# The second layer's heads in groups of two pairs instead of pair by pair

## The chip, the cores and the metric

The kernel runs on one core of a Trainium2 chip. The metric is the device time of one execution in microseconds. Before the change three runs gave 348.47, 349.83 and 350.31; their median is 349.83 us.

## The reference, cut to what matters

Two layers work on 256 tokens of width 1024, all in 32-bit floats. The first layer (a state-space half and a gated linear attention half) is the same before and after. The second layer is this, with 16 heads of width 64; with 256 tokens there is a single block of keys, so what is left of the block-sparse attention is ordinary causal attention:

```python
def moba_layer(x, norm_w, w_in, w_out):
    h = rms_norm(x, norm_w)
    u = h @ w_in                              # 1024 x 4096
    q, k, v, z = split_cols(u, (1024,) * 4)   # 16 heads of 64 each
    s = (q * 64 ** -0.5) @ k.T                # by head, 256 x 256
    p = softmax(where(key <= query, s, -inf))
    o = (p @ v) * silu(z)                     # silu(z) is the gate
    return x + o @ w_out                      # then a last rms_norm
```

## The kernel before, in words

A product of two 32-bit matrices is made of three fast ones: each operand is split into a high part in a reduced 32-bit format (`h_...`, `...hi`) and a low rest (`l_...`, `...lo`), and `mm3` (line 161) queues high x high, high x low and low x high into the same sum. A weight piece of 128 x 1024 numbers comes by one DMA, is split by ScalarE (high part, line 78) and VectorE (rest, line 79), and is then used once. There are four buffers for raw pieces and seven for split ones; pieces are fetched in the order of a list, `pieces`.

Eight pairs of heads are worked on in turn (`for pr in range(8)`). A pair has three projection blocks of 24 matmuls each, written to tiles called `pp`: q, k, and the gate z. After q and k, a generator `co_attn` is started for the pair. It runs beside the projections: `yield 2600` means that its next step is queued when TensorE has been given another 2600 ns of work by the program's own count (`spend`, `due`). The order on TensorE's queue is thus fixed when the program is built. The steps of `co_attn` are:

- scores, tiles `as`: one head of the pair uses the upper 64 rows of the 128 x 128 array and the other the lower 64 rows, so the two run side by side. The first 128 queries are multiplied in full precision, the others by three fast products.
- on VectorE the masked row minimum (line 710), on ScalarE the exponential (line 712), on VectorE the reciprocal of the sum and the rescaling (lines 714 and 716);
- transposes of the probabilities, tiles `ptp`: six full-array matmuls against a unit matrix, copied to `pT` by ScalarE (line 724);
- products with the values, tile `ao`: each head uses 64 columns of the array. VectorE multiplies with the gate (`og`, line 735), ScalarE and VectorE split the result into `oghi` and `oglo` (lines 736 and 737), which are row block `pr` of the last projection's input.

The last projection (tiles `pf`) adds up eight such row blocks. For three of its four tiles the first seven blocks (`lead`) are queued before the generators are drained, the eighth afterwards. In PSUM, `pp` and `pf` share four banks, and the mixers' tiles `as`, `ptp` and `ao` four others.

The lines that do the two steps in question are

```python
for j, r in enumerate(rows):                                   # rows: 0-63, 64-127
    mm(sps[j][:, 0:P], qt[0][r, 0:P], kt[0][r, 0:P])           # scores, full precision
for i, (a_, b_) in enumerate(((1, 1), (1, 2), (2, 1))):
    for j, r in enumerate(rows):
        mm(sps[j][:, P:3 * P], qt[a_][r, :], kt[b_][r, :], i == 0, i == 2)
...
for j, r in enumerate(rows):
    mm(ops[r, 0:T], va[:, 0, hc[j]], pTs[j][:, 0:T], True, False)
```

A full-precision matmul has two records in the trace, a fast one has one.

Of the kernel before, what the change touches and what calls it, by code (L numbers as in the profile page):

```python
# [35 lines left out]
# columns of the packed constants  # L36
# [4 lines left out]
# columns of the packed matrices of shape  # L41
# [5 lines left out]
def trunk(ctx, tc, xT_d, x_d, cst_d, mat_d, gw2_d, fn_d, wa_d, wb_d, wc_d, wv_d, wp_d, wf_d, out_d):  # L47
# [21 lines left out]
    # ------------------------------------------------------------------ weights  # L69
# [50 lines left out]
    for j in range(24):  # L120
        plan(("p", j), wp_d[j], KB, P)
# [49 lines left out]
    # keep the tensor engine's clock up until the first operands arrive  # L171
    warm = cpool.tile([P, T], F32R, name="warm")
# [5 lines left out]
    # ------------------------------------------------------------------ inputs  # L178
# [3 lines left out]
    gw2 = cpool.tile([16, 512], F32, name="gw2")  # L182
# [68 lines left out]
    # ------------------------------------------------------------------ even in-projection  # L251
# [65 lines left out]
    def co_first(ps):  # L317
# [12 lines left out]
        # softplus of the step sizes, by the series of artanh  # L330
# [31 lines left out]
        # gate logits -> cumulated log decay (times 16)  # L362
# [18 lines left out]
    # convolution and silu  # L381
# [74 lines left out]
    # gated linear attention  # L456
# [126 lines left out]
    # ------------------------------------------------------------------ gate of the state-space half  # L583
# [37 lines left out]
    # ------------------------------------------------------------------ even out-projection  # L621
# [13 lines left out]
    def gemm_tt(name, hi8, lo8, tag):  # L635
        """Token-major product, one token tile after the other: yields each when it is done."""
# [46 lines left out]
    # ------------------------------------------------------------------ second layer  # L683
# [12 lines left out]
    def co_attn(pr, qt, kt, ops):  # L696
        yield DL["at0"]
        sps = [pm(f"as{pr}_{j}") for j in range(2)]
        for j, r in enumerate(rows):
            mm(sps[j][:, 0:P], qt[0][r, 0:P], kt[0][r, 0:P])  # L700
        for i, (a_, b_) in enumerate(((1, 1), (1, 2), (2, 1))):
            for j, r in enumerate(rows):
                mm(sps[j][:, P:3 * P], qt[a_][r, :], kt[b_][r, :], i == 0, i == 2)
        pts = [tmp.tile([P, 3 * P], F32, name=f"pt{pr}_{j}", tag="t1d") for j in range(2)]
        for j in range(2):
            pt = pts[j]
            nm = sm.tile([P, 2], F32, name=f"nm{pr}_{j}", tag="nm")
            sme = sm.tile([P, 2], F32, name=f"sme{pr}_{j}", tag="sme")
            for tt, cs in halves:
                V.tensor_tensor_reduce(out=pt[:, cs], in0=sps[j][:, cs], in1=mask[:, cs], scale=rq[:, tt:tt + 1],  # L710
                                       scalar=3e38, op0=ALU.add, op1=ALU.min, accum_out=nm[:, tt:tt + 1])
                S.activation(pt[:, cs], pt[:, cs], AF.Exp, scale=-1.0, bias=nm[:, tt:tt + 1],
                             accum_out=sme[:, tt:tt + 1])
            V.reciprocal(sme, sme)
            for tt, cs in halves:
                V.tensor_scalar(pt[:, cs], pt[:, cs], sme[:, tt:tt + 1], None, op0=ALU.mult)
        yield DL["at2"]
        pTs = []
        for j in range(2):
            tp = pm(f"ptp{pr}_{j}")  # L720
            for i in range(3):
                tr(tp[:, i * P:i * P + P], pts[j][:, i * P:i * P + P])
            pT = tmp.tile([P, 3 * P], F32, name=f"pT{pr}_{j}", tag="t3")
            S.activation(pT, tp[:, 0:3 * P], AF.Copy)
            pTs.append(pT)
        yield DL["at3"]
        hc = [slice(64 * (2 * pr + j), 64 * (2 * pr + j) + 64) for j in range(2)]
        for j, r in enumerate(rows):
            mm(ops[r, 0:T], va[:, 0, hc[j]], pTs[j][:, 0:T], True, False)
        for j, r in enumerate(rows):  # L730
            mm(ops[r, P:T], va[:, 1, hc[j]], pTs[j][:, T:3 * P], False, True)
        while ("z", pr) not in env:
            yield 300
        og = tmp.tile([P, T], F32, name=f"og{pr}", tag="t1f")
        V.tensor_tensor(og, ops[:, 0:T], env[("z", pr)], op=ALU.mult)
        S.activation(oghi[:, pr, :], og, AF.Copy)
        V.tensor_sub(oglo[:, pr, :], og, oghi[:, pr, :].bitcast(F32))

    for pr in range(8):
        qk = []  # L740
        for i in range(2):
            ps = gemm_fm(("p", 3 * pr + i), h1hi, h1lo, f"pp{pr}_{i}")
            t_ = tmp.tile([P, T], F32, name=f"qk{pr}_{i}", tag=("t1a", "t1c")[i])
            n_ = (P, T)[i]
            hi = big.tile([P, n_], F32R, name=f"qkh{pr}_{i}", tag=(("cbT0", "cbT1"), ("qs", "ks"))[i][pr % 2])
            lo = big.tile([P, n_], F32R, name=f"qkl{pr}_{i}", tag=(("s3", "s4"), ("bc", "gs"))[i][pr % 2])
            if i == 0:
                S.activation(t_[:, 0:P], ps[:, 0:P], AF.Copy)
                S.activation(hi, ps[:, P:T], AF.Copy)
                V.tensor_sub(lo, ps[:, P:T], hi.bitcast(F32))  # L750
            else:
                V.tensor_tensor(t_, ps, rb1, op=ALU.mult)
                S.activation(hi, t_, AF.Copy)
                V.tensor_sub(lo, t_, hi.bitcast(F32))
            qk.append((t_, hi, lo))
        ops = pm(f"ao{pr}")
        spawn(co_attn(pr, *qk, ops))
# [134 lines left out]
```

## Time and profile before

| what | value |
|---|---|
| median of three runs | 349.83 us |
| span of the profiled execution | 347.5 us |
| TensorE busy (matmuls) | 335.5 us, 97% of the span |
| VectorE busy | 263.5 us, 76% |
| ScalarE busy | 217.5 us, 63% |
| HBM read | 54.63 MB, 160 GB/s over the span |
| share of the chain that ended last on TensorE | 85% |
| of it projections of the second layer (`pp`) | 21% |

The span runs from the first to the last instruction of the profiled execution; the profile has no time for that execution beyond its span. A matmul's record begins when its operands are being fetched and lasts longer than its place in the queue, so records of neighbours overlap, and what a matmul costs is read from the distance between starts. PE is TensorE, DVE VectorE, ACT ScalarE. A row such as `128*64` gives the rows and columns of the array that a matmul uses.

### The profile page before, as it was taken

How to read it: one execution, taken by the hardware profiler on the slowest of the kernel's cores; microseconds unless marked ns; L12 is line 12 of the kernel's file. 1: busy time of each engine (PE TensorE's matmuls, PEld its weight loads, DVE VectorE, ACT ScalarE, POOL GpSimd, SP SyncE). 2: the span in 40 equal slices, each digit the busy share in tenths (PEclk: the TensorE clock that was granted, in tenths of full speed). 3: DMA queues.
4: the chain of work that ended last, by engine and by line, in shares of the span. 5: the costliest groups of instructions: out<-in, count | busy, mean ns of one | idle time of the engine just before them, and what ended most of it. 6: DMA issues, size and time to landing. Idle time of an engine off the chain costs nothing.

```text
span 347.5 us, 6341 instructions
## 1 busy us (share of the span) xinstructions
PE 335.5 (97%) x2352; PEld 305.2 (88%) x2352; DVE 263.5 (76%) x548; ACT 217.5 (63%) x445; POOL 49.3 (14%) x62
## 2 busy tenths in 40 slices
PE   8699999999999999999999999999999999999992
PEld 7599989998999899999888888899999999998792
DVE  5979999999989658789974775377777877777243
ACT  5547689898765757577542676466657665674222
POOL 2610001112415442434200000000000000000000
PEclk9999999999999999999999999999999999999998
DMA  7778672365573745631685634766344335430003
GB/s 209 238 245 283 219 255 94 80 185 178 162 227 115 252 132 170 186 117 41 207 296 189 201 121 163 241 210 214 124 158 146 123 122 183 122 123 0 3 0 121
DMA packets 17631, 56.09 MB, mean 161 GB/s; under 512 B 2096, under 2 KB 4144, under 8 KB 17472
## 3 DMA queue, kind: packets, MB, share of 16 engines
q1 hardware_dynamic: 16880, 53.53, 47.7%
q10 hardware_dynamic: 720, 2.16, 1.8%
q8 instruction: 18, 0.29, 0.4%
q14 instruction: 13, 0.11, 0.1%
HBM read 54.63 MB, written 1.05 MB: 160 GB/s over the span
## 4 chain that ended last, share of the span: by engine, by line
PE 85%; DVE 5%; issue 3%; DMA 2%; POOL 2%; SPq 0%; ACT 0%; POOLq 0%; DVEq 0%
PE pp L158 21%; PE pb L158 18%; PE pc L158 13%; PE pa L158 11%; PE pv L158 6%; PE pf L158 4%; DMA r_a<-in_wa 2%; PE ao L158 2%; PE yp L158 2%; PE as L158 2%; PE ptp L162 2%; PE gs L158 1%; PE go L158 1%; POOL rr L537 1%; POOL sT L517 1%
## 5 line engine op out<-in xcount | busy, mean ns | idle before, releaser
L158 PE MATMUL pb<-hhi,h_b 128*128 128x256 f32 x208 | 60.0, 288 | 0.0
L158 PE MATMUL pb<-hlo,h_b 128*128 128x256 f32 x208 | 58.7, 282 | 0.0
L158 PE MATMUL pb<-hhi,l_b 128*128 128x256 f32 x208 | 58.7, 282 | 0.0
L158 PE MATMUL pp<-h1hi,h_p 128*128 128x256 f32 x192 | 56.3, 293 | 0.0
L158 PE MATMUL pp<-h1lo,h_p 128*128 128x256 f32 x192 | 54.2, 282 | 0.0
L158 PE MATMUL pp<-h1hi,l_p 128*128 128x256 f32 x192 | 54.2, 282 | 0.0
L158 PEld LDWEIGHTS pb<-hhi,h_b 128*128 128x128 f32 x208 | 39.7, 191 | 1.2 <-issue 1.1
L158 PEld LDWEIGHTS pb<-hlo,h_b 128*128 128x128 f32 x208 | 39.7, 191 | 0.0
L158 PEld LDWEIGHTS pb<-hhi,l_b 128*128 128x128 f32 x208 | 39.7, 191 | 0.0
L79 DVE TENSOR_TENSOR l_p<-r_p,h_p 128x1024 fp32r<-128x1024 f32 x24 | 29.4, 1225 | 12.2 <-ACT h_p L78 11.6
L158 PEld LDWEIGHTS pp<-h1hi,h_p 128*128 128x128 f32 x192 | 36.6, 191 | 2.1 <-issue 1.0
L158 PEld LDWEIGHTS pp<-h1lo,h_p 128*128 128x128 f32 x192 | 36.6, 191 | 0.0
L158 PEld LDWEIGHTS pp<-h1hi,l_p 128*128 128x128 f32 x192 | 36.6, 191 | 0.0
L78 ACT ACTIVATE h_b<-r_b 128x1024 fp32r<-128x1024 f32 x26 | 27.4, 1067 | 9.5 <-DMA r_b<-in_wb 5.3
L79 DVE TENSOR_TENSOR l_b<-r_b,h_b 128x1024 fp32r<-128x1024 f32 x26 | 31.3, 1214 | 1.8 <-ACT h_b L78 1.8
L158 PE MATMUL pa<-l_a,hhi 128*128 128x416 f32 x80 | 28.4, 354 | 3.0 <-DVE l_a L79 3.0
L78 ACT ACTIVATE h_p<-r_p 128x1024 fp32r<-128x1024 f32 x24 | 25.3, 1056 | 9.5 <-PE pp L158 5.4
L158 PE MATMUL pa<-h_a,hhi 128*128 128x416 f32 x80 | 29.0, 363 | 0.1
L158 PE MATMUL pa<-h_a,hlo 128*128 128x416 f32 x80 | 28.2, 353 | 1.0 <-DVE hlo L215 1.0
L79 DVE TENSOR_TENSOR l_a<-r_a,h_a 128x832 fp32r<-128x832 f32 (+1 forms) x24 | 22.8, 960 | 2.2 <-ACT h_a L78 2.2
L79 DVE TENSOR_TENSOR l_c<-r_c,h_c 128x1024 fp32r<-128x1024 f32 x16 | 19.9, 1252 | 4.8 <-ACT h_c L78 4.8
L78 ACT ACTIVATE h_c<-r_c 128x1024 fp32r<-128x1024 f32 x16 | 16.9, 1056 | 10.1 <-DMA r_c<-in_wc 6.3
(241 smaller groups left out, 804.4 us busy)
## 6 DMA issues: line engine op xcount, KB each, us to landing
r_b<-in_wb SPq DMA_DIRECT2D x26, 512.0 KB, 4.2
r_p<-in_wp SPq DMA_DIRECT2D x24, 512.0 KB, 4.0
r_c<-in_wc SPq DMA_DIRECT2D x16, 512.0 KB, 4.2
r_a<-in_wa SPq DMA_DIRECT2D x16, 416.0 KB, 3.6
r_v<-in_wv SPq DMA_DIRECT2D x8, 512.0 KB, 4.5
r_f<-in_wf SPq DMA_DIRECT2D x8, 512.0 KB, 3.5
r_a<-in_wa SPq DMA_DIRECT2D x8, 208.0 KB, 3.6
xT<-in_xT SPq DMA_DIRECT2D x8, 128.0 KB, 3.6
```

The costliest lines, as they stand in the source:

```text
L78: S.activation(hi, raw, AF.Copy)
L79: V.tensor_sub(lo, raw, hi.bitcast(F32))
L158: TE.matmul(out, lhsT, rhs, start=start, stop=stop)
L162: TE.transpose(out, in_, ident)
L517: G.affine_select(out=sT[:, 0:3:2, :], in_=sT[:, 0:3:2, :], pattern=[[0, 2], [1, P]], compare_op=ALU.is_ge, fill=0.0, base=0, channel_mult ...
L537: G.tensor_tensor(rr, ss, mhalf, op=ALU.pow)
```

## The change

Two pairs form a group, and there are four groups. The weight list and the projections of a group go q, k, q, k, gate, gate. One generator serves the group: it queues the scores of both pairs one after the other, then the softmax of the four heads, then the transposes of the first pair, later those of the second pair, and then the products with the values of both pairs into one tile `ao`. The waiting counts are changed with it (5000 instead of 4350 before the first transposes, 3700 between the two, 1800 before the products as it was). The probabilities of a group lie in one buffer in the place of `v`, and `pT` in two single buffers; the gate has a second buffer. To make room, two small tiles of the first layer (`warm`, `gw2`) share memory with others. Of the last projection six row blocks instead of seven are queued before the drain.

```diff
-      "turn": 4150, "rb1": 4000, "at0": 2600, "at2": 4350, "at3": 1800, "gqk": 250}
+      "turn": 4150, "rb1": 4000, "at0": 2600, "at2": 5000, "at1": 3700, "at3": 1800, "gqk": 250}
...
-    for j in range(24):
-        plan(("p", j), wp_d[j], KB, P)
+    for g in range(4):
+        for j in (0, 1, 3, 4, 2, 5):
+            plan(("p", 6 * g + j), wp_d[6 * g + j], KB, P)
...
-    warm = cpool.tile([P, T], F32R, name="warm")
+    warm = big.tile([P, T], F32R, name="warm", tag="s0")
...
-    gw2 = cpool.tile([16, 512], F32, name="gw2")
+    gw2 = big.tile([16, 512], F32, name="gw2", tag="s4")
...
-    def co_attn(pr, qt, kt, ops):
+    def co_attn(g, qks):
+        prs = (2 * g, 2 * g + 1)
         yield DL["at0"]
+        sps = {}
+        for pr, (qt, kt) in zip(prs, qks):
             for j, r in enumerate(rows):
+                sps[pr, j] = pm(f"as{pr}_{j}")
+                mm(sps[pr, j][:, 0:P], qt[0][r, 0:P], kt[0][r, 0:P])
+            for i, (a_, b_) in enumerate(((1, 1), (1, 2), (2, 1))):
+                for j, r in enumerate(rows):
+                    mm(sps[pr, j][:, P:3 * P], qt[a_][r, :], kt[b_][r, :], i == 0, i == 2)
+        ptb = big.tile([P, 4, 3 * P], F32, name=f"pt{g}", tag="v")
...
         yield DL["at2"]
+        for n, pr in enumerate(prs):
+            pTb = big.tile([P, 2, 3 * P], F32, name=f"pT{pr}", tag=f"s{n}")
+            for j in range(2):
+                tp = pm(f"ptp{pr}_{j}")
+                for i in range(3):
+                    tr(tp[:, i * P:i * P + P], pts[pr, j][:, i * P:i * P + P])
+                pTs[pr, j] = pTb[:, j, :]
+                S.activation(pTs[pr, j], tp[:, 0:3 * P], AF.Copy)
+            yield DL["at1"] if pr == prs[0] else DL["at3"]
+        ops = pm(f"ao{g}")
+        for n, pr in enumerate(prs):
+            hc = [slice(64 * (2 * pr + j), 64 * (2 * pr + j) + 64) for j in range(2)]
+            for j, r in enumerate(rows):
+                mm(ops[r, n * T:n * T + T], va[:, 0, hc[j]], pTs[pr, j][:, 0:T], True, False)
+            for j, r in enumerate(rows):
+                mm(ops[r, n * T + P:n * T + T], va[:, 1, hc[j]], pTs[pr, j][:, T:3 * P], False, True)
...
-    for pr in range(8):
+    for g in range(4):
+        qks = []
+        for pr in (2 * g, 2 * g + 1):
...
+        spawn(co_attn(g, qks))
+        for pr in (2 * g, 2 * g + 1):
+            ps = gemm_fm(("p", 3 * pr + 2), h1hi, h1lo, f"pp{pr}_2")
...
-    lead = range(KB - 1)
+    lead, rest = range(KB - 2), (KB - 2, KB - 1)
...
-        part(pf[n, 0], f"f{n}", oghi, oglo, 0, (KB - 1,), ("f0", 3))
+        part(pf[n, 0], f"f{n}", oghi, oglo, 0, rest, ("f0", 3))
```

In the order of the instructions, TensorE first, at the scores of pair 2 before (`as_0` and `as_1` are the two heads, `qk` the full-precision operands, `qkh` and `qkl` their high and low parts; a name's last number is a buffer):

```order
L158 MATMUL pp_2_3109<-h1hi,l_p_2945 128x256
L158 MATMUL as_0_3136<-qk_1_3096,qk_0_3047 128x128
L158 MATMUL as_1_3137<-qk_1_3096,qk_0_3047 128x128
L158 MATMUL as_0_3136<-qkh_1_3097,qkh_0_3048 128x256
L158 MATMUL as_1_3137<-qkh_1_3097,qkh_0_3048 128x256
L158 MATMUL as_0_3136<-qkl_1_3098,qkh_0_3048 128x256
L158 MATMUL as_1_3137<-qkl_1_3098,qkh_0_3048 128x256
L158 MATMUL as_0_3136<-qkh_1_3097,qkl_0_3049 128x256
L158 MATMUL as_1_3137<-qkh_1_3097,qkl_0_3049 128x256
L158 MATMUL pp_2_3109<-h1hi,h_p_2944 128x256
```

The same engine at the scores of pairs 2 and 3 in the changed kernel, from the last step of pair 2 on (3227 and 3229 are pair 2's tiles, 3237 and 3239 pair 3's):

```order
L159 MATMUL as_0_3227<-qkh_1_3071,qkl_0_3024 128x256
L159 MATMUL as_1_3229<-qkh_1_3071,qkl_0_3024 128x256
L159 MATMUL as_0_3237<-qk_1_3172,qk_0_3118 128x128
L159 MATMUL as_1_3239<-qk_1_3172,qk_0_3118 128x128
L159 MATMUL as_0_3237<-qkh_1_3173,qkh_0_3119 128x256
L159 MATMUL as_1_3239<-qkh_1_3173,qkh_0_3119 128x256
L159 MATMUL as_0_3237<-qkl_1_3174,qkh_0_3119 128x256
L159 MATMUL as_1_3239<-qkl_1_3174,qkh_0_3119 128x256
L159 MATMUL as_0_3237<-qkh_1_3173,qkl_0_3120 128x256
L159 MATMUL as_1_3239<-qkh_1_3173,qkl_0_3120 128x256
L159 MATMUL pp_2_3220<-h1hi,h_p_3078 128x256
```

Pair 3's first product follows pair 2's last one directly, where a projection matmul stood before. The group's products with the values stand alike: a pair's four instructions stood between two projection matmuls, and now eight do. Here they are in the changed kernel:

```order
L159 MATMUL pp_1_3130<-h1hi,l_p_2994 128x256
L159 MATMUL ao_3143<-pT_3041,va 64x256 x2
L159 MATMUL ao_3143<-pT_3041,va 64x128 x2
L159 MATMUL ao_3143<-pT_3101,va 64x256 x2
L159 MATMUL ao_3143<-pT_3101,va 64x128 x2
L159 MATMUL pp_1_3130<-h1hi,h_p_2993 128x256
```

`pT_3041` belongs to the first pair of the group and `pT_3101` to the second. In all, `as` and `ao` are each queued in four places instead of eight, and `ptp` in eight as before. In one place of the kernel before, the products of pair 0 and the scores of pair 1 already stood side by side.

VectorE before, from the first reduction of pair 3's scores (`ISA`, with the row minimum `nm`) to its last rescaling (`TENSOR_SCALAR`); `zs` is the gate, `l_p` a weight split:

```order
L710 ISA pt_0_3307,nm_0_3309<-as_0_3297,mat,rq 128x128
...
L710 ISA pt_1_3308,nm_1_3318<-as_1_3298,mat,rq 128x256
L710 ISA nm_1_3318 128x1
L761 SCALAR_TENSOR_TENSOR zs_3334<-pp_2_3270,rb_2337 128x256
L79 TENSOR_TENSOR l_p_3502<-r_p_3499,h_p_3501 128x1024
L714 RECIPROCAL sme_0_3310<-sme_0_3310 128x2
L714 RECIPROCAL sme_1_3319<-sme_1_3319 128x2
L716 TENSOR_SCALAR pt_0_3307<-pt_0_3307,sme_0_3310 128x128
L716 TENSOR_SCALAR pt_0_3307<-pt_0_3307,sme_0_3310 128x256
L716 TENSOR_SCALAR pt_1_3308<-pt_1_3308,sme_1_3319 128x128
L716 TENSOR_SCALAR pt_1_3308<-pt_1_3308,sme_1_3319 128x256
```

VectorE in the changed kernel, from the last reduction of pair 2's scores to its last rescaling (3237 is pair 3's first head):

```order
L719 ISA pt_3247,nm_1_3257<-as_1_3229,mat,rq 128x256
L719 ISA nm_1_3257 128x1
L723 RECIPROCAL sme_0_3249<-sme_0_3249 128x2
L719 ISA pt_3247,nm_0_3266<-as_0_3237,mat,rq 128x128
...
L725 TENSOR_SCALAR pt_3247<-pt_3247,sme_0_3249 128x128
L725 TENSOR_SCALAR pt_3247<-pt_3247,sme_0_3249 128x256
L723 RECIPROCAL sme_1_3258<-sme_1_3258 128x2
L719 ISA pt_3247,nm_0_3266<-as_0_3237,mat,rq 128x256
...
L725 TENSOR_SCALAR pt_3247<-pt_3247,sme_1_3258 128x128
L725 TENSOR_SCALAR pt_3247<-pt_3247,sme_1_3258 128x256
```

Two reductions of pair 3's first head now stand before pair 2's last rescaling, and the gate and the weight split stand behind it. The rows of SP and GpSimd are the same in both kernels, and the first layer's order is the same on every engine.

## Rows read from the trace of the kernel before

**Rows 1.** The page: busy us (share of the span) xinstructions of each engine.

```profile
PE 335.5 (97%) x2352; PEld 305.2 (88%) x2352; DVE 263.5 (76%) x548; ACT 217.5 (63%) x445; POOL 49.3 (14%) x62
```

**Rows 2.** Who PE waited for, whole span: us in total, times, longest us.

```profile
PE pa L158 <- DVE l_a L79: 3.0, 3, 2.0
```

**Rows 3.** Busy us by stretch: its length, PE, PEld, DVE, ACT, POOL, clock, DMA, GB/s.

```profile
229.00:317.00 88.00, 88.00 (x756) 82.87 (x755) 67.32 (x180) 54.72 (x135) 0.00 (x0) 1.00 0.46 149
317.00:341.00 24.00, 23.90 (x135) 20.12 (x133) 11.11 (x30) 8.46 (x23) 0.55 (x1) 1.00 0.05 19
```

**Rows 4.** Timeline of PE, one pair: start us, length us, line, operation, tiles, count.

```profile
267.81 0.28 PE L158 MATMUL pp<-h1hi,l_p 128*128 128x256 f32 x1
268.02 0.87 PE L158 MATMUL ao<-pT,va 128*64 128x256 f32 x8
268.82 0.39 PE L158 MATMUL pp<-h1hi,h_p 128*128 128x256 f32 x1
...
270.23 0.28 PE L158 MATMUL pp<-h1hi,l_p 128*128 128x256 f32 x1
270.44 0.49 PE L158 MATMUL as<-qk,qk 64*128 64x128 f32 x4
...
270.89 0.28 PE L158 MATMUL as<-qkl,qkh 64*128 64x256 f32 x2
271.00 0.28 PE L158 MATMUL as<-qkh,qkl 64*128 64x256 f32 x2
271.21 0.39 PE L158 MATMUL pp<-h1hi,h_p 128*128 128x256 f32 x1
...
272.63 0.28 PE L158 MATMUL pp<-h1hi,l_p 128*128 128x256 f32 x1
...
276.23 0.28 PE L158 MATMUL pp<-h1hi,l_p 128*128 128x256 f32 x1
276.35 0.82 PE L162 MATMUL ptp<-mat,pt 128*128 128x128 f32 x6
276.92 0.36 PE L158 MATMUL pp<-h1hi,h_p 128*128 128x256 f32 x1
277.12 0.28 PE L158 MATMUL pp<-h1lo,h_p 128*128 128x256 f32 x1
```

**Rows 5.** Timeline of PE where pair 0's products meet pair 1's scores.

```profile
247.21 0.87 PE L158 MATMUL ao<-pT,va 128*64 128x256 f32 x8
248.01 0.49 PE L158 MATMUL as<-qk,qk 64*128 64x128 f32 x4
...
248.79 0.39 PE L158 MATMUL pp<-h1hi,h_p 128*128 128x256 f32 x1
```

**Rows 6.** Timeline of PE in the first layer, 64-row products in sequence.

```profile
116.68 0.49 PE L158 MATMUL gs<-e,e 64*128 64x128 f32 x4
117.00 0.39 PE L158 MATMUL gs<-qs,ks 64*128 64x128 f32 x4
117.23 0.77 PE L158 MATMUL gs<-e,e 64*128 64x128 f32 x12
```

**Rows 7.** VectorE's reductions of the scores: ns least/median/most, first and last start.

```profile
L710 DVE CUSTOM_DVE_ANT_0 pt<-as,mat,rq x32: 344/414/481, 240.3 to 317.1; 128x128 f32<-128x128 f32 x16, 128x256 f32<-128x256 f32 x16
```

**Rows 8.** Timeline of DVE after pair 3's scores.

```profile
273.25 1.22 DVE L79 TENSOR_TENSOR l_p<-r_p,h_p 128x1024 fp32r<-128x1024 f32 x1 [0.15 <-ACT h_p L78]
...
274.70 0.99 DVE L716 TENSOR_SCALAR pt<-pt,sme 128x128 f32<-128x128 f32 x4
```

**Rows 9.** Timeline of PE in the last projection.

```profile
318.27 0.39 PE L158 MATMUL pf<-h_f,oghi 128*128 128x512 f32 x1
...
320.54 0.39 PE L158 MATMUL pf<-l_f,oghi 128*128 128x512 f32 x1
```

**Rows 10.** Timeline of DVE in the last projection.

```profile
324.73 0.42 DVE L735 TENSOR_TENSOR og<-ao,zs 128x256 f32<-128x256 f32 x1 [3.85 <-PE ao L158]
...
326.20 0.42 DVE L737 TENSOR_TENSOR oglo<-og,oghi 128x256 fp32r<-128x256 f32 x1
```

More of the change, by code (lines that the diff above doesn't have):

```diff
@@ L694, in trunk @@
     halves = ((0, slice(0, P)), (1, slice(P, 3 * P)))
-    def co_attn(pr, qt, kt, ops):
+    def co_attn(g, qks):
+        prs = (2 * g, 2 * g + 1)
         yield DL["at0"]
[L698 to L701, printed above, removed]
+        sps = {}
+        for pr, (qt, kt) in zip(prs, qks):
             for j, r in enumerate(rows):
[L703 to L716, printed above, removed]
-        yield DL["at2"]
[L718 to L732, printed above, removed]
-            yield 300
[L734 to L737, printed above, removed]
@@ L739, in trunk @@
-    for pr in range(8):
[L740 to L757, printed above, removed]
-        ps = gemm_fm(("p", 3 * pr + 2), h1hi, h1lo, f"pp{pr}_2")
-        th = tmp.tile([P, T], F32, name=f"mth{pr}", tag="t1b")
-        zs = tmp.tile([P, T], F32, name=f"zs{pr}", tag="t1e")
-        V.scalar_tensor_tensor(zs, ps, 0.5, rb1, op0=ALU.mult, op1=ALU.mult)
-        S.activation(th, zs, AF.Tanh)
-        V.scalar_tensor_tensor(zs, th, 1.0, zs, op0=ALU.add, op1=ALU.mult)
-        env[("z", pr)] = zs
@@ new lines, in co_attn @@
+                sps[pr, j] = pm(f"as{pr}_{j}")
[4 more added lines that the diff above has]
+        ptb = big.tile([P, 4, 3 * P], F32, name=f"pt{g}", tag="v")
+        pts, pTs = {(pr, j): ptb[:, 2 * n + j, :] for n, pr in enumerate(prs) for j in range(2)}, {}
+        for pr in prs:
+            for j in range(2):
+                sp_ = sps[pr, j]
+                pt = pts[pr, j]
+                nm = sm.tile([P, 2], F32, name=f"nm{pr}_{j}", tag="nm")
+                sme = sm.tile([P, 2], F32, name=f"sme{pr}_{j}", tag="sme")
+                for tt, cs in halves:
+                    V.tensor_tensor_reduce(out=pt[:, cs], in0=sp_[:, cs], in1=mask[:, cs], scale=rq[:, tt:tt + 1],
+                                           scalar=3e38, op0=ALU.add, op1=ALU.min, accum_out=nm[:, tt:tt + 1])
+                    S.activation(pt[:, cs], pt[:, cs], AF.Exp, scale=-1.0, bias=nm[:, tt:tt + 1],
+                                 accum_out=sme[:, tt:tt + 1])
+                V.reciprocal(sme, sme)
+                for tt, cs in halves:
+                    V.tensor_scalar(pt[:, cs], pt[:, cs], sme[:, tt:tt + 1], None, op0=ALU.mult)
@@ new lines, in co_attn @@
+        yield DL["at2"]
+        for n, pr in enumerate(prs):
+            pTb = big.tile([P, 2, 3 * P], F32, name=f"pT{pr}", tag=f"s{n}")
+            for j in range(2):
+                tp = pm(f"ptp{pr}_{j}")
[5 more added lines that the diff above has]
+        ops = pm(f"ao{g}")
@@ new lines, in co_attn @@
+        for n, pr in enumerate(prs):
[4 more added lines that the diff above has]
+                mm(ops[r, n * T + P:n * T + T], va[:, 1, hc[j]], pTs[pr, j][:, T:3 * P], False, True)
+        while ("z", prs[1]) not in env:
+            yield 300
+        for n, pr in enumerate(prs):
+            og = tmp.tile([P, T], F32, name=f"og{pr}", tag="t1f")
+            V.tensor_tensor(og, ops[:, n * T:n * T + T], env[("z", pr)], op=ALU.mult)
+            S.activation(oghi[:, pr, :], og, AF.Copy)
+            V.tensor_sub(oglo[:, pr, :], og, oghi[:, pr, :].bitcast(F32))
@@ new lines, in trunk @@
+    for g in range(4):
+        qks = []
+        for pr in (2 * g, 2 * g + 1):
+            qk = []
+            for i in range(2):
+                ps = gemm_fm(("p", 3 * pr + i), h1hi, h1lo, f"pp{pr}_{i}")
+                t_ = tmp.tile([P, T], F32, name=f"qk{pr}_{i}", tag=("t1a", "t1c")[i])
+                n_ = (P, T)[i]
+                hi = big.tile([P, n_], F32R, name=f"qkh{pr}_{i}", tag=(("cbT0", "cbT1"), ("qs", "ks"))[i][pr % 2])
+                lo = big.tile([P, n_], F32R, name=f"qkl{pr}_{i}", tag=(("s3", "s4"), ("bc", "gs"))[i][pr % 2])
+                if i == 0:
+                    S.activation(t_[:, 0:P], ps[:, 0:P], AF.Copy)
+                    S.activation(hi, ps[:, P:T], AF.Copy)
+                    V.tensor_sub(lo, ps[:, P:T], hi.bitcast(F32))
+                else:
+                    V.tensor_tensor(t_, ps, rb1, op=ALU.mult)
+                    S.activation(hi, t_, AF.Copy)
+                    V.tensor_sub(lo, t_, hi.bitcast(F32))
+                qk.append((t_, hi, lo))
+            qks.append(qk)
+        spawn(co_attn(g, qks))
+        for pr in (2 * g, 2 * g + 1):
+            ps = gemm_fm(("p", 3 * pr + 2), h1hi, h1lo, f"pp{pr}_2")
+            th = tmp.tile([P, T], F32, name=f"mth{pr}", tag="t1b")
+            zs = tmp.tile([P, T], F32, name=f"zs{pr}", tag=("t1e", "t1g")[pr % 2])
+            V.scalar_tensor_tensor(zs, ps, 0.5, rb1, op0=ALU.mult, op1=ALU.mult)
+            S.activation(th, zs, AF.Tanh)
+            V.scalar_tensor_tensor(zs, th, 1.0, zs, op0=ALU.add, op1=ALU.mult)
+            env[("z", pr)] = zs
@@ L803, in trunk @@
     finish(0, sf[:, 0:1], ssf[:, 0, 1:2])
-    part(pf[0, 1], "f0", oghi, oglo, 1, (KB - 1,), ("f0", 3))
+    part(pf[0, 1], "f0", oghi, oglo, 1, rest, ("f0", 3))
     add_res(0, 512, 1, pf[0, 1], 0)
```

## The prediction, made before the changed kernel ran

> **What bounds the kernel now.** I read the page's engine list first, then TensorE's waits, then the stretch of the change, then TensorE's timeline inside it. TensorE is busy 97% of the span, VectorE 76%, ScalarE 63% [rows 1]. The list of what TensorE waited for has three entries, the largest of 3.0 us in total [rows 2]; all three name tiles of the warm-up or of the first layer's token projection, none a tile of the second layer. In the 88 us in which the heads of the second layer run, and in the last projection behind them, TensorE has no idle time at full clock, while VectorE is busy 67.3 of 88 us [rows 3]. So every microsecond that TensorE's queue loses there reaches the end, unless something new makes it wait; and nothing that only relieves VectorE, ScalarE or a DMA can show.
>
> Inside the stretch the question is what TensorE's own steps cost. Projection matmuls (pp) follow each other at 0.12 us: 30 of them from 272.63 to 276.23 take 3.60 [rows 4]. The 24 projection blocks of 24 matmuls each are the same before and after, so this part is constant. Around the mixers' steps the spacing changes. The last pp before the products with the values (ao, half-width arrays of 64 columns) starts 0.21 before them instead of 0.12; ao lasts 0.80 to the next pp; from there to 270.23 there are 11 steps that take 1.41 instead of 1.32. So one visit to ao costs 0.09 + 0.80 + 0.09 = 0.98 us [rows 4]. The scores (as, arrays of 64 rows) likewise: 0.09 before (270.23 to 270.44), 0.77 of their own, and 0.10 behind (11 steps from 271.21 to 272.63 take 1.42): 0.96 [rows 4]. The transposes (ptp, full array) pay nothing for coming and going: from 276.23 to 277.12 is 0.89 us, less two pp steps of 0.12 leaves 0.65 for six, 0.11 each [rows 4]. So it is the change of the array's shape that costs, some 0.18 to 0.19 a visit outside and some more at the first and last step inside, and the ptp visits, which stay eight, need no price. The account closes: 576 x 0.12 + 8 x 0.96 + 7 x 0.98 + 7 x 0.65 (pair 7's last two visits come later), less 0.18 for the one visit that two shared [rows 5], is 88.0, and the stretch is 88.0 long [rows 3].
>
> **The change part by part.**
>
> *Visits.* Before, eight visits of as and eight of ao; now four and four, twice as long. Once before, ao and as already stood side by side: pair 0's products and pair 1's scores, 247.21 to 248.79 [rows 5]. That is 15 trips away from the projections before, 8 after: 7 x 0.185 = 1.30 us saved. In that one case ao still lasts 0.80 and as 0.78 [rows 5], since the shape changes between them; only the outer part was shared.
>
> *The seam inside a double visit to the scores.* Its last step on the way out is 0.21 (271.00 to 271.21) where the step before it, of the same shape and width, is 0.11 (270.89 to 271.00) [rows 4]. Between two pairs of the same shape I take 0.12: 0.09 saved. The first step of the second pair is a full-precision 64-row product, and a seam where such a product follows the three of the fast 32-bit kind (256 columns each) is not in this trace. What is there is the first layer: the first four records of such products take 0.32 (116.68 to 117.00), the next four, of other tiles but the same shape, 0.23 (117.00 to 117.23) [rows 6]: 0.09 to 0.10 saved. Together 0.19 x 4 = 0.76.
>
> *The seam inside a double visit to the products.* Two 256-column and two 128-column record pairs; at the spacing of [rows 6], 0.11 to 0.115 a pair of 128 columns, they stream in 2 x 0.22 + 2 x 0.11 = 0.66, against 0.80 alone [rows 4]: 0.14 x 4 = 0.56.
>
> Nothing in the trace makes a seam dearer than leaving and coming back, so the bound below is that both seam terms are zero (the sum is then 1.30) and above it the full 2.62; below the streaming time a seam cannot go. I take the full value, since [rows 6] is the same shape on the same engine and [rows 4] shows the same inside a visit.
>
> The Trainium skill speaks against that in "TensorE: Matmul & The Clock Gate", section "Part 3: Packing small matmuls": weight loads overlap matmuls in flight only where the row group differs. At the seam the row groups are the same, so by it each of the eight seams would show a weight load; with 0.10 for each, the visible part of a first load in [rows 6], the sum would be 1.8 and not 2.62. The trace does not follow that rule inside a visit: the scores' step from 270.89 to 271.00, whose weights go to the row group in use, is no longer than a pp step [rows 4]. No run here shows the seam itself, so it has its part in a rival below.
>
> *The softmax chain.* Eight reductions now come at once, 0.41 us each [rows 7], and the rescaling of the second pair's heads, the gate product and a weight split stand behind. Before, pair 3's scores were done at 271.21 and its last rescaling at 275.69 (274.70 + 0.99), 4.5 us, including a split of 1.2 in VectorE's queue [rows 4, 8]; its transposes came at 276.35 [rows 4]. Now two reductions of the other pair (0.8 us) stand in front of the first pair's last rescaling, and the split and the gate product no longer do. Even if these had saved nothing that is 5.3 us; TensorE is given 48 pp steps, 5.76 us, before it transposes. I cost it at nothing. The second pair has 36 steps more.
>
> *Buffers and banks.* Four score tiles take all four banks of their pool, so the next group's scores need the last ao tile read; 42 pp steps (5.0 us) lie between, and og begins 0.12 after ao. The probabilities have one buffer instead of two; its next writing is a whole group later. The moves of warm and gw2 into shared memory and the weights' order change no queue of the first layer, nor any row of SP or GpSimd. Nothing for all of these.
>
> *The end.* Two pairs instead of one now finish late, so two row blocks wait behind the lead instead of one. Between the last products and their first use stood 36 matmuls, now 12; at 0.227 (ten from 318.27 to 320.54) that is 2.7 us [rows 9]. Before, the low half was done 1.9 us after og began, with a split of 1.2 in VectorE's queue between (324.73 to 326.20 + 0.42) [rows 10]. A second og and a second subtraction make it 2.7 if a split still lies there, 1.5 if not. Zero to 0.4 us of wait; I take zero, as the split now stands ahead of og.
>
> **Sum.** 1.30 + 0.76 + 0.56 = 2.62 us off TensorE. The profiled span is 347.5, the median of the runs shown 349.83, so 2.33 lie outside the span and are kept. 347.5 - 2.6 + 2.3 = 347.2 us, 0.75% less. What comes late next is again TensorE: after the change the nearest thing behind it is the tail above.
>
> **Rivals.**
>
> *The seam is paid.* The array waits at the seam as it does on leaving or coming, or shows the second pair's first weight load. For it: the seam from the fast 32-bit kind to full precision in the 64-row shape is in no row. Against: [rows 6] and the 0.11 steps in [rows 4]. The price is 8 x 0.10 for the loads (0.32 against 0.23 in [rows 6]) up to both seam terms, 1.32: 348.0 to 348.5, middle 348.3.
>
> *The gain is hidden.* A share of the visits' cost is only order in the records, or a wait just behind TensorE takes its place, such as the 12-matmul cover of the end or a weight that arrives later: the time stays within 1 us of 349.8. Against: TensorE has no idle time anywhere in the stretch [rows 3], and its account closes without a rest.
>
> *Slower: the burst on VectorE.* TensorE reaches the first transposes before the rescaling is done, four times. If the second pair's whole chain stood ahead of them, VectorE would have eight reductions (8 x 0.41 = 3.3) [rows 7], eight rescalings (2 x 0.99 = 2.0) and a split (1.2) [rows 8], and the gate's two steps, in the shape of og (2 x 0.42 = 0.8) [rows 10]: 7.3 us against a cover of 5.76, 1.5 x 4 = 6.2 us lost, 353.4. It decides for slower from 1.1 us a group ((2.6 + 1.75) / 4), so from a chain of 6.9 us. Against: in the new order only two of the second pair's reductions stand there.
>
> **How the numbers follow.** Forecast 0.68; seam paid 0.17; hidden 0.09; burst 0.06. Under 0.5% of 349.83, 1.75 us, this kernel's runs (348.47 to 350.31) can hardly tell a change from none, so faster needs under 348.1. Of the forecast I give nine tenths to that, of the seam rival a third, of the hidden one a tenth: 0.61 + 0.06 + 0.01 = 0.68; slower is the burst and a little of the hidden: 0.06; same 0.26. The forecast's own range is 346.3 to 348.0; the tenth above is reached inside the hidden case at 349.2, the tenth below at 346.0.
>
> **What would show it.** In the profile after: as in four visits of about 1.35 us with 0.12 and 0.11 at the seam; ao in four of about 1.46; TensorE without idle time from the first pp to its last matmul, and that matmul some 2.6 us earlier. A seam of 0.2 us shows the first rival; a wait of ptp for VectorE or of pf for the last pairs' halves the others. The prediction is wrong if TensorE's end moves by less than 1.8 us or the time behind its last matmul grows.

## The result and the profile after

The changed kernel takes 347.13 us (median of nine runs, 345.89 to 347.97); the kernel before took 349.83 us in the same rounds (nine runs, 348.35 to 351.14). The ratio is 0.9931, with a 95% interval of 0.9911 to 0.9951. The forecast was 347.2 us, with a range of 346.0 to 349.2.

The profiled execution of the changed kernel has a span of 344.2 us, against 347.5. In the program's listing of the changed kernel every helper has moved by one line (`mm` is L159 now). Its engine line on the page, to be read beside [rows 1]:

```profile
PE 334.2 (97%) x2352; PEld 306.3 (89%) x2352; DVE 262.4 (76%) x548; ACT 217.4 (63%) x445; POOL 51.3 (15%) x62
```

The number of instructions that the page counts is the same on every engine, and TensorE is busy 1.3 us less, in a span that is 3.3 us shorter (it also waited less in the first layer, so its busy time alone doesn't show the gain). The list of what TensorE waited for (total us, times, longest us) answers to [rows 2]:

```profile
PE pa L159 <- DVE l_a L79: 1.3, 2, 0.7
PE warmp L177 <- DVE mhalf L200: 1.3, 1, 1.3
PE pb L159 <- DVE l_b L79: 0.8, 1, 0.8
```

All three are in the first layer or its warm-up; no tile of the second layer is there. So nothing of the change's own stretch has become a wait, and the 3.3 us have to be looked for in two places: the stretch, and what lies ahead of it. The windows of the changed kernel from its first second-layer projection matmul (first pp) to the start of its last matmul, and from there to the end (length, PE, PEld, DVE, ACT, POOL, clock, DMA, GB/s):

```profile
228.17:337.31 109.14, 109.14 (x888) 102.49 (x887) 77.54 (x208) 62.86 (x156) 0.55 (x1) 1.00 0.39 125
337.31:344.17 6.86, 0.28 (x3) 0.07 (x1) 1.46 (x4) 1.23 (x3) 0.55 (x1) 0.81 0.20 76
```

The same two windows of the kernel before:

```profile
228.96:340.62 111.66, 111.66 (x888) 102.95 (x887) 78.16 (x207) 63.18 (x156) 0.55 (x1) 1.00 0.37 120
340.62:347.48 6.86, 0.28 (x3) 0.07 (x1) 1.71 (x7) 1.23 (x3) 0.55 (x1) 0.76 0.30 113
```

The stretch has 888 matmul records in both, no idle time in either, and is 111.66 - 109.14 = 2.52 us shorter. The tail is 6.86 us in both. The other 0.79 us (228.96 - 228.17) was gained before the stretch began, in a first layer whose instructions did not change; the last section shows that this part differs by as much between profiles of one program. So 2.52 us is the change's, and the 0.79 can't be put down to it.

Inside the stretch the timeline of TensorE shows one double visit to the scores and one to the products in the changed kernel (start us, length us, line, operation, tiles, count), to be read beside [rows 4]:

```profile
258.24 0.28 PE L159 MATMUL pp<-h1hi,l_p 128*128 128x256 f32 x1
258.45 1.52 PE L159 MATMUL ao<-pT,va 128*64 128x256 f32 x16
259.90 0.39 PE L159 MATMUL pp<-h1hi,h_p 128*128 128x256 f32 x1
...
264.92 0.28 PE L159 MATMUL pp<-h1hi,l_p 128*128 128x256 f32 x1
265.13 0.49 PE L159 MATMUL as<-qk,qk 64*128 64x128 f32 x4
265.38 0.37 PE L159 MATMUL as<-qkh,qkh 64*128 64x256 f32 x2
265.58 0.28 PE L159 MATMUL as<-qkl,qkh 64*128 64x256 f32 x2
265.70 0.28 PE L159 MATMUL as<-qkh,qkl 64*128 64x256 f32 x2
265.81 0.39 PE L159 MATMUL as<-qk,qk 64*128 64x128 f32 x4
265.95 0.37 PE L159 MATMUL as<-qkh,qkh 64*128 64x256 f32 x2
266.15 0.29 PE L159 MATMUL as<-qkl,qkh 64*128 64x256 f32 x2
266.27 0.29 PE L159 MATMUL as<-qkh,qkl 64*128 64x256 f32 x2
266.50 0.38 PE L159 MATMUL pp<-h1hi,h_p 128*128 128x256 f32 x1
```

Read the starts, not the lengths: the array is pipelined, and what a step costs is the distance to the next start. The seam between the two pairs' scores is at 265.70 to 265.81, 0.11 us; the same step at the way out is 0.23 (266.27 to 266.50). The first group of the second pair takes 0.14 (265.81 to 265.95), that of the first pair 0.25 (265.13 to 265.38). A double visit lasts 1.37 here, where two single ones lasted 2 x 0.77; one to the products lasts 1.45, where two lasted 2 x 0.80.

### The profile page after: what moved, and what is told of

Its sections match the earlier page's. It is cut to its first block, busy times and chain, and to the rows that moved or that the text cites. A ratio compares the mean times of both kernels' runs of the same rounds, so it can differ in the third digit from the quotient of the medians.

```text
span 344.2 us, 6316 instructions
## 1 busy us (share of the span) xinstructions
PE 334.2 (97%) x2352; PEld 306.3 (89%) x2352; DVE 262.4 (76%) x548; ACT 217.4 (63%) x445; POOL 51.3 (15%) x62
## 4 chain that ended last, share of the span: by engine, by line
PE 85%; DVE 4%; issue 4%; DMA 3%; POOL 2%; ACT 1%; SPq 1%; POOLq 0%; DVEq 0%
PE pp L159 20%; PE pb L159 18%; PE pc L159 13%; PE pa L159 11%; PE pv L159 6%; PE pf L159 4%; DMA r_a<-in_wa 3%; PE yp L159 2%; PE ao L159 2%; PE as L159 2%; PE ptp L163 2%; PE gs L159 1%; PE go L159 1%; POOL rr L538 1%; POOL sT L518 1%
## 5 line engine op out<-in xcount | busy, mean ns | idle before, releaser
L159 PE MATMUL pb<-hhi,h_b 128*128 128x256 f32 x208 | 60.0, 288 | 0.0
L159 PE MATMUL pb<-hhi,l_b 128*128 128x256 f32 x208 | 58.9, 283 | 0.8 <-DVE l_b L79 0.8
L159 PE MATMUL pb<-hlo,h_b 128*128 128x256 f32 x208 | 58.8, 282 | 0.0
L159 PE MATMUL pp<-h1hi,h_p 128*128 128x256 f32 x192 | 55.5, 289 | 0.0
L159 PE MATMUL pp<-h1lo,h_p 128*128 128x256 f32 x192 | 54.3, 283 | 0.0
L159 PE MATMUL pp<-h1hi,l_p 128*128 128x256 f32 x192 | 54.3, 283 | 0.0
L159 PEld LDWEIGHTS pb<-hhi,h_b 128*128 128x128 f32 x208 | 39.7, 191 | 1.2 <-issue 1.1
L159 PEld LDWEIGHTS pb<-hhi,l_b 128*128 128x128 f32 x208 | 39.8, 191 | 1.0 <-DVE l_b L79 1.0
L159 PEld LDWEIGHTS pb<-hlo,h_b 128*128 128x128 f32 x208 | 39.8, 191 | 0.0
L159 PEld LDWEIGHTS pp<-h1hi,h_p 128*128 128x128 f32 x192 | 36.7, 191 | 1.1 <-issue 0.5
L159 PEld LDWEIGHTS pp<-h1lo,h_p 128*128 128x128 f32 x192 | 36.8, 192 | 0.0
L159 PEld LDWEIGHTS pp<-h1hi,l_p 128*128 128x128 f32 x192 | 36.7, 191 | 0.0
L79 DVE TENSOR_TENSOR l_b<-r_b,h_b 128x1024 fp32r<-128x1024 f32 x26 | 33.0, 1276 | 1.8 <-ACT h_b L78 1.8
L159 PE MATMUL pa<-l_a,hhi 128*128 128x416 f32 x80 | 28.9, 361 | 1.3 <-DVE l_a L79 1.3
L159 PE MATMUL pa<-h_a,hhi 128*128 128x416 f32 x80 | 29.6, 370 | 0.0
L159 PE MATMUL pa<-h_a,hlo 128*128 128x416 f32 x80 | 28.7, 359 | 0.0
L78 ACT ACTIVATE h_a<-r_a 128x832 fp32r<-128x832 f32 (+1 forms) x24 | 18.7, 783 | 8.0 <-DMA r_a<-in_wa 6.5
```

Source lines behind the costliest of these rows:

```text
L78: S.activation(hi, raw, AF.Copy)
L79: V.tensor_sub(lo, raw, hi.bitcast(F32))
L159: TE.matmul(out, lhsT, rhs, start=start, stop=stop)
```

## The experiments

All are edits of the changed kernel. The yardstick is the stretch, from the start of the first pp to the start of the last matmul: in the changed kernel it was 109.139 us in both of its two profiles, and in all experiments but one TensorE reached the stretch 190.3 us after the first layer's convolution tile `acp`, as before. The median of a whole run scatters by as much as most of these effects.

**Scores of the two pairs apart, all else as changed.** The theory says that each split scores visit gives back an outer trip and the inner seam; the rival that the gain is hidden says that nothing happens.

```diff
                     mm(sps[pr, j][:, P:3 * P], qt[a_][r, :], kt[b_][r, :], i == 0, i == 2)
+            if pr == prs[0]:
+                yield 600
```

> The changed kernel, but six projection matmuls stand between the scores of the two pairs of a group; products stay together. Theory (the visits and the seam make the gain): each of the four visits becomes two of 0.77 us with 0.18 to 0.19 around the second, so the first layer-two projection matmul to the last matmul takes 4 x (0.18 + 0.185) = 1.46 us more than the 109.14 of the changed kernel, 110.6, and the time is about 348.6. Rival (the order of the projections, the longer waiting counts or the buffers make the gain): 109.1 and 347.1, as changed.

Measured: stretch 110.659, so 1.52 us more; median 348.31 us, ratio to the kernel before 0.9964 (0.9944 to 0.9984). The timeline of this kernel at the way out of the first pair's scores and at the way into the second's:

```profile
267.23 0.28 PE L159 MATMUL as<-qkh,qkl 64*128 64x256 f32 x2
267.44 0.39 PE L159 MATMUL pp<-h1hi,h_p 128*128 128x256 f32 x1
267.66 0.28 PE L159 MATMUL pp<-h1lo,h_p 128*128 128x256 f32 x1
...
268.14 0.28 PE L159 MATMUL pp<-h1hi,l_p 128*128 128x256 f32 x1
268.35 0.49 PE L159 MATMUL as<-qk,qk 64*128 64x128 f32 x4
268.59 0.37 PE L159 MATMUL as<-qkh,qkh 64*128 64x256 f32 x2
```

The four prices of a trip are all back: 0.21 at the way out (0.11 at the seam), 0.22 for the first pp behind it (0.12 among pp's), 0.21 for the pp ahead of the next visit (0.12), and 0.24 for the first group (0.14).

**Products of the two pairs apart.**

```diff
                 mm(ops[r, n * T + P:n * T + T], va[:, 1, hc[j]], pTs[pr, j][:, T:3 * P], False, True)
+            if n == 0:
+                yield 600
```

> The changed kernel, but six projection matmuls stand between the products with the values of the two pairs of a group; scores stay together. Theory: each visit of 1.45 us becomes two of 0.80 with 0.18 around the second: 4 x (0.15 + 0.18) = 1.32 us more, 110.5 for the stretch and about 348.5. Rival (as above): 109.1 and 347.1.

Measured: stretch 110.432, 1.29 us more, as expected. The median, 347.19 us (ratio 0.9934, 0.99 to 0.9969), does not show it: it was expected 1.3 us higher, and that part of the expectation failed. The span of its profile is 345.3 us, 1.1 above the changed kernel's, with a start that was 0.2 us earlier (first pp at 228.0). Four of its five timed runs have the higher mean clock of the last section (0.994 to 0.998). Of the two measurements the stretch is the one that can tell 1.3 us.

**Both apart.**

> The changed kernel with scores and products of every pair apart by six projection matmuls: 16 visits again, but in the new order, with its counts, buffers and lead. Theory: all of the gain goes, and the one shared visit of the kernel before as well: 109.14 + 1.46 + 1.32 = 111.9 for the stretch against 111.66 before, about 349.9, the same as before. Rival (order, counts or buffers): stays near 347.1.

Measured: stretch 111.953, 2.81 us more, which is 1.52 + 1.29 to the hundredth; median 349.01 us, ratio 0.999 (0.9969 to 1.001). With both steps split again the whole gain is gone, though the order q k q k gate gate, the grouping, the shared buffers and the single late drain of two row blocks are all still there. So the gain is the trips', and the rest of the change is worth nothing by itself. That it is even 0.29 us above the kernel before is mostly the one place where that kernel had a products visit and a scores visit side by side ([rows 5]), which saves a trip of 0.18.

**What the seam costs if the array's shape changes there.** One matmul of the full array, whose result is not used, between the two pairs' scores:

```diff
+            if pr == prs[0]:
+                mm(sps[pr, 0][:, 3 * P:4 * P], h1hi[:, 0, 0:P], h1hi[:, 0, 0:P])
```

> The changed kernel with one more matmul of the full array (128 columns, fast kind, its result not used) between the scores of the two pairs of a group. Theory (a change of the array's shape costs): a visit to the scores, from its first record to the next projection matmul, grows from 1.364 us by the 0.18 of the seam, by about 0.18 for going to the full shape and back, and by 0.06 to 0.12 for the matmul itself: 1.79 to 1.85. Rival (the cost is one of leaving the queue's pattern, of the first weight load behind any other work): the same growth as in the run with an extra matmul of 64 rows at that place.

Measured: the double visit lasts 1.804 instead of 1.364, and the stretch 110.952, 1.81 us more (4 x 0.44 and 0.05 elsewhere). The timeline of this kernel at the seam:

```profile
266.28 0.28 PE L159 MATMUL as<-qkh,qkl 64*128 64x256 f32 x2
266.49 0.33 PE L159 MATMUL as<-h1hi 128*128 128x128 f32 x1
266.75 0.49 PE L159 MATMUL as<-qk,qk 64*128 64x128 f32 x4
267.00 0.37 PE L159 MATMUL as<-qkh,qkh 64*128 64x256 f32 x2
```

One small matmul takes 0.26 itself and makes the step ahead of it 0.21 and the group behind it 0.25, the very prices of leaving and coming.

**The same with more work of the 64-row shape.** Two products of the shape in use, of 128 columns, at the same place, their results not used either:

```diff
+            if pr == prs[0]:
+                for j, r in enumerate(rows):
+                    mm(sps[pr, j][:, 3 * P:4 * P], qt[1][r, :], kt[1][r, 0:P])
```

> The changed kernel with one more pair of matmuls of 64 rows (128 columns, fast kind, result not used) between the scores of the two pairs of a group. Theory (only a change of the array's shape costs): a visit to the scores grows by the pair's own place alone, 0.06 to 0.12 us, from 1.364 to 1.42 to 1.48. Rival (any other work in the seam exposes a load or a drain): it grows by 0.25 or more.

Measured: the double visit lasts 1.464, 0.10 more than without them; stretch 109.592. The timeline at the seam:

```profile
266.81 0.28 PE L159 MATMUL as<-qkh,qkl 64*128 64x256 f32 x2
266.93 0.23 PE L159 MATMUL as<-qkh,qkh 64*128 64x128 f32 x2
266.99 0.44 PE L159 MATMUL as<-qk,qk 64*128 64x128 f32 x4
267.18 0.37 PE L159 MATMUL as<-qkh,qkh 64*128 64x256 f32 x2
```

The added pair takes 0.06 and the seam stays at 0.12 (266.81 to 266.93), but the group behind the pair takes 0.19 (266.99 to 267.18) where it took 0.14; why is not shown. Still, most of the 0.44 that the full-array matmul cost is neither the number of matmuls nor a weight load into a row group that is in use: it is the change of shape. The Trainium skill states this in "TensorEngine Tiling (Array Packing)", section "Key Properties": changing the tiling mode, and not just the tile, drains TensorE. These two runs agree in that a change of mode is what costs, 0.44 against 0.10 a visit; that it is a drain they do not show, and the page gives no price.

**The cover of the softmax cut.** To see how far the first pair's rescaling was from becoming a wait, TensorE was given 1500 ns of work in place of 5000 between the scores and the first transposes:

```diff
-      "turn": 4150, "rb1": 4000, "at0": 2600, "at2": 5000, "at1": 3700, "at3": 1800, "gqk": 250}
+      "turn": 4150, "rb1": 4000, "at0": 2600, "at2": 1500, "at1": 3700, "at3": 1800, "gqk": 250}
```

> The changed kernel with 1500 instead of 5000 as the count between scores and first transposes, so 15 projection matmuls (1.9 us) instead of 48 (5.8) cover the softmax of the first pair. Theory (VectorE's and ScalarE's chain was hidden; in the changed kernel it ends 3.8 us after the scores): the transposes wait, the second head's until about 3.9 us after the scores, so some 1.7 us a group are lost, 4 x 1.7 = 6.8 us, span about 351. If the chain were no limit: 344.2.

Measured: stretch 115.573, 6.43 us more; 353.55 us in the one run. The list of TensorE's waits in this kernel now leads with the rival's:

```profile
PE ptp L163 <- DVE pt L725: 3.5, 8, 0.6
```

Eight waits, two in each group. The list counts idle time only from the modelled end of the matmul before, so it shows 3.5 us of the loss. The steps show all of it: in every group the last pp before the transposes takes 0.91 to 0.92 us instead of 0.12, and the first visit to them 1.41 instead of 0.57, 6.5 us in all. So TensorE can reach the transposes before the rescaling is done, as the slower rival has it, and the cover of 48 pp's is what kept that away.

**The products beside the next scores.** If a trip between shapes is what costs, the products of one group can be queued right ahead of the next group's scores, and share a trip three times:

```diff
         yield DL["at0"]
+        if "products" in env:
+            env.pop("products")()
...
-        ops = pm(f"ao{g}")
...
+        def products():
+            ops = pg(f"ao{g}")
...
+        if g < 3:
+            env["products"] = products
+        else:
+            products()
```

> The changed kernel, but the products of a group are queued right before the scores of the next group, in a bank of the projections' pool (group 3's as before). Theory: three trips away from the projections are shared, the shape still changes between products and scores, so only the outer part is saved: 3 x 0.18 = 0.55 us, 108.6 for the stretch and about 346.6. Rival (two kinds in one visit share nothing, or the later products make TensorE wait): 109.1 or more.

Measured: stretch 108.572, 0.57 us less than the changed kernel, as expected; median 346.63 us, ratio to the kernel before 0.991 (0.9884 to 0.9936). Since 0.5 us is within the scatter of the medians, this version and the changed kernel were run once more in the same rounds:

> The changed kernel once more, on the same chip as the next one and the kernel before. If its first profile is typical, the time from the first pp of the second layer to the last matmul is again 109.14 us (before 111.66) and the median is near 347.1; the rest of the span, whose first layer is unchanged, can differ by about a us between profiles.

> The version with the products of a group beside the next group's scores, once more: 108.57 us from the first pp to the last matmul, 0.57 less than the changed kernel, and a median 0.5 us below the changed kernel's in the same rounds. If the gain of 0.5 us in the whole time is lost in the start of the kernel, the two medians stand within 0.3 us of each other and only the stretch shows it.

Measured: the changed kernel 346.05 us (six runs, ratio 0.9901, 0.9881 to 0.9921), stretch 109.139; the side-by-side version 346.92 us (six runs, ratio 0.991, 0.9886 to 0.9933), stretch 108.579. The timeline of the side-by-side version, where the products run into the scores:

```profile
265.27 0.28 PE L159 MATMUL pp<-h1hi,l_p 128*128 128x256 f32 x1
265.48 1.52 PE L159 MATMUL ao<-pT,va 128*64 128x256 f32 x16
266.93 0.49 PE L159 MATMUL as<-qk,qk 64*128 64x128 f32 x4
```

The stretch is shorter by the three trips in both profiles (0.57 and 0.56), and the median is not: over all runs it lies between the two medians of the changed kernel. The part ahead of the stretch decides which of them looks faster. So this version does beat both kernels in the part that it changes, and whether a whole execution is shorter is not shown.

**The same idea in the first layer.** There, products called yp use 64 columns for one block at a time, eight visits. Two blocks were held back and multiplied together, in four visits. The operands got a third buffer, and to make room the tile `yacc` shares memory with another; those lines are not shown:

```diff
         yield DL["pair1"]
+        held.append((blk, xdt, e))
+        if len(held) < 2:
+            return
         yp = pm(f"yp{blk}")
...
+        for i, (_, xd, ee) in enumerate(held):
+            for j, r in enumerate(rows):
+                mm(yp[r, i * T:i * T + T], xd[:, 0, j, :], ee[:, j, 0:2, :].rearrange("p a b -> p (a b)"), True, False)
```

> The changed kernel, and in the first layer the products of two blocks of the state-space half (yp, arrays of 64 columns, eight visits of 0.80 us) are queued together in four visits; a third buffer for their operands. Theory: the same price per visit as in the second layer's products, 4 x 0.33 = 1.3 us off the first layer, less what two visits shared with other narrow ones already; about 345.8. Rival (the later blocks of y or the buffers make TensorE, VectorE or ScalarE wait there): no gain or slower.

Measured: a miss. The median is 347.3 us (ratio 0.9942, 0.992 to 0.9963). The stretch is unchanged at 109.139, and the time from `acp` to the first pp is 190.93 instead of 190.32: 0.6 more where 1.3 less was expected. The double visits do last 1.45, as in the second layer, and all steps of yp together take 5.80 instead of 6.41. But the list of TensorE's waits has two new entries:

```profile
PE obt L163 <- DVE ob L548: 0.8, 1, 0.8
PE xtp L163 <- DVE y L459: 0.3, 1, 0.3
```

The second is the held block's: two y's come to VectorE in one piece, and TensorE stood still for them. The first comes 30 us after the last double visit (obt at 156.02). VectorE's timeline shows what stood ahead of the `ob` that it waited for:

```profile
153.90 0.42 DVE L598 SCALAR_TENSOR_TENSOR zu<-pb,rb 128x256 f32<-128x256 f32 x1
154.24 1.22 DVE L79 TENSOR_TENSOR l_c<-r_c,h_c 128x1024 fp32r<-128x1024 f32 x1
155.37 1.12 DVE L548 SCALAR_TENSOR_TENSOR ob<-go,rr,gs 128x128 f32<-128x128 f32 x4
```

A weight split of 1.22 us has come between zu and ob; in the changed kernel ob follows zu directly, and TensorE does not wait. So the order on VectorE's queue, which the program does not fix as it does TensorE's, shifted with the edit. These 1.1 us, and steps around the linear attention's products that became longer (1.59 instead of 1.25 at one place), outweigh the trips. The waits are shown; how the rest divides was not tried.

## Why the prediction was right, step by step

The starts of successive matmul records, summed by tile over the stretch, give the account (us):

| tile | before | after | difference |
|---|---|---|---|
| pp | 72.117 | 70.839 | -1.278 |
| as | 6.191 | 5.456 | -0.735 |
| ao | 6.406 | 5.804 | -0.602 |
| ptp | 4.584 | 4.588 | +0.004 |
| pf and the last tile | 22.361 | 22.452 | +0.091 |
| stretch | 111.659 | 109.139 | -2.520 |

- *Visits*, forecast 7 x 0.185 = 1.30. The step into a shape costs 0.089 above a pp's, and the steps behind it 0.090, 0.179 together: 7 x 0.179 = 1.25. The term was right and 0.05 too large, since 0.185 came from two digits.
- *The seam in the scores*, forecast 0.76: measured 0.735. Its two halves are as the prediction put them: the way out 0.21 to 0.23 against 0.11 at the seam, the first group 0.25 against 0.14.
- *The seam in the products*, forecast 0.56: measured 0.60. So the first layer's products in [rows 6] gave the right measure for a seam that the trace before did not have. The prediction calls them the same shape; they use 64 rows and `ao` uses 64 columns, so for the products it was a measure borrowed from another shape, and it held.
- *The transposes*, for which the prediction took no price. Its reading that they pay nothing for coming and going is not right: six take 0.57 us (276.35 to 276.92), and the step behind their first pp is 0.20 (276.92 to 277.12 [rows 4]), nearly the 0.22 behind the scores. It did no harm, since all eight visits stay. But the transposes use the full array, so that part of a trip is not the mark of a change of shape alone. What remains of the account is 0.07 us: the steps behind the mixers' visits cost that much more in all, most of it because one of the transposes' visits has moved from among the pp's to among the pf's. This and the visits' 0.05 make up the 0.10 by which 2.62 was too much; the errors of the two seams nearly cancel.
- *The softmax chain*, forecast at no more than 5.3 us against a cover of 5.76. VectorE's timeline in the changed kernel, behind scores that ended at 266.50:

```profile
268.56 0.35 DVE L719 CUSTOM_DVE_ANT_0 pt<-as,mat,rq 128x128 f32<-128x128 f32 x1
...
269.40 0.47 DVE L719 CUSTOM_DVE_ANT_0 pt<-as,mat,rq 128x256 f32<-128x256 f32 x1
...
269.79 0.54 DVE L725 TENSOR_SCALAR pt<-pt,sme 128x128 f32<-128x128 f32 x2
...
273.50 0.55 DVE L725 TENSOR_SCALAR pt<-pt,sme 128x128 f32<-128x128 f32 x2
```

  The two reductions of the second pair at 268.56 and 269.40 do stand ahead of the first pair's last rescaling, as forecast; it ends at 270.33, 3.8 us after the scores, and the transposes begin at 272.35, 2.0 us later (1.8 to 2.0 in the four groups). The bound of 5.3 was safe and 1.5 too long, because the split and the gate no longer stood in front. The second pair's ends at 274.05.
- *Buffers and banks*, forecast at nothing: no wait in the stretch.
- *The end*, forecast at zero of 0 to 0.4 us. VectorE's timeline in the changed kernel, in the last projection:

```profile
324.86 0.76 DVE L747 TENSOR_TENSOR og<-ao,zs 128x256 f32<-128x256 f32 x2 [3.93 <-PE ao L159]
325.76 0.76 DVE L749 TENSOR_TENSOR oglo<-og,oghi 128x256 fp32r<-128x256 f32 x2 [0.15 <-ACT oghi L748]
329.16 0.69 DVE L788 TENSOR_TENSOR x<-x,pf 128x512 f32<-128x512 f32 x1 [2.63 <-PE pf L159]
```

  Both low halves are done at 326.52, 1.7 us after og began, near the 1.5 that was worked out for a queue without a split, and 1.1 us before the first pf that uses them (327.60, behind the 12 pf's); VectorE waits for TensorE again at 329.16, not the other way round.

The rivals fell each by a run. *Seam paid*: the seam is 0.11 to 0.12, not 0.21, and stays there with more work of the same shape. So the rule on weight loads of the Trainium skill ("TensorE: Matmul & The Clock Gate", section "Part 3: Packing small matmuls"), by which each seam would have shown a load, does not decide here: the row groups at the seam are the same, and no load shows. *Gain hidden*: splitting both visits again gives back the full 2.81 us. *Burst on VectorE*: TensorE waits with a count of 1500 and not with one of 5000.

One thing in the number was luck. The forecast took 2.62 us off the span and added 2.33 around it, and so came within 0.1 us of the median. The 2.33 are not all time outside the span: in the runs that list both, the time is 1.7 to 1.8 us above the span, and the other 0.6 is the distance between the profiled execution and the median. The sum is thus the median before less 2.62. And medians of this kernel in two sessions are 347.13 and 346.05, those of the kernel before 349.83 and 349.89. The mechanism is settled by the stretch, to some hundredths; the median alone could have come out 1 us lower for the same reason.

## What to carry to other kernels

When TensorE has no idle time, look at the distances between the starts of its matmuls: steps of another array shape cost 0.18 us for coming and going and another 0.15 to 0.18 at their own first and last step, so put together what has the same shape. Whether that pays depends on the cover of what then comes late in a burst: in the second layer there were 2 us to spare, in the first layer TensorE came to wait for VectorE, and the same idea lost time. Judge an effect of a few tenths of a per cent by the stretch that was changed, measured within one trace, before trusting the medians of whole runs.

## What was not expected of the hardware

The scatter of a whole execution is made in its first 40 us. The time from the first matmul of the first layer to `acp` lies between 32.0 and 34.1 us, for instructions whose order no edit touched. In five of the twelve profiles the granted clock falls to half (1.2 of 2.4 GHz) for 3.4 us, some 10 to 14 us after it first rose; in the others it stays at full until the end. The window of the side-by-side version's first profile where it happens (length, PE, PEld, DVE, ACT, POOL, clock, DMA, GB/s):

```profile
17.50:20.90 3.40, 3.40 (x12) 3.23 (x11) 2.71 (x4) 1.06 (x1) 0.20 (x1) 0.50 0.92 286
```

and the same window of the kernel before:

```profile
17.50:20.90 3.40, 2.73 (x16) 2.72 (x17) 3.40 (x5) 1.06 (x1) 0.17 (x1) 1.00 0.73 237
```

Twelve records instead of sixteen, with TensorE busy all the while instead of partly waiting for its input. Just before the dip TensorE had waited 1.84 us for a weight split (l_a) and was busy for 1.56 us from 14.10 to 17.50; the kernel before has such a wait too (2.0 us, [rows 2]) and no dip, so the wait alone does not bring it about. The five profiles with the dip need 33.2 to 34.1 us to `acp`, the seven without it 32.0 to 33.0. In the changed kernel's fifteen timed runs the mean clock of the execution falls in two groups that fit this: 0.989 to 0.991 in six runs of 347.13 to 347.97 us, and 0.994 to 0.998 in nine of 345.81 to 346.44. The kernel before has the lower clock (0.985 to 0.993) in 31 of the 44 runs of the experiments' sessions. Compared within a group, the medians of the two kernels differ by 2.2 us at the lower clock (349.9 and 347.7) and by 2.9 at the higher (348.9 and 346.0), on either side of the stretch's 2.5; the 3.8 us between the medians of the second session, 349.89 and 346.05, hold the mix of the groups as well. What brings the dip about was not tried, nor whether the change makes it rarer, through the new place of `warm` for instance, nor whether the side-by-side version, eight of whose ten runs have a clock of 0.989 to 0.992, meets it more often by cause or by chance.
